# Gates of two token tiles: one-hot products, or added slot by slot into tables in DRAM

## The chip, the cores and the metric

The kernel runs on one core of one Trainium2 chip. A core has five engines with their own instruction queues: TensorE (PE), VectorE (DVE), ScalarE (ACT), GpSimd (POOL) and SyncE (SP), which only issues DMA transfers. ACT and POOL issue transfers too. All move through the core's 16 DMA engines. What counts is the time of one execution in microseconds on the device.

## The reference, cut to what matters

One decoder block over 1024 tokens of width 1024: a mixer made of two gated linear recurrences, then a PEER expert layer, then a norm. The change is in the expert layer. Each token picks, in each of 8 heads, 16 of 16,384 single-neuron experts, so it has 128 slots, each with an expert number and a gate:

```
s_top, i_top = lax.top_k(s, PEER_TOPK)
cand = s_top[:, :, 0, :, None] + s_top[:, :, 1, None, :]
cand_idx = i_top[:, :, 0, :, None] * PEER_N_KEYS + i_top[:, :, 1, None, :]
...
g = jax.nn.softmax(best, axis=-1)
act = jax.nn.gelu(jnp.einsum('td,thkd->thk', xb, u[expert]), approximate=False)
return jnp.einsum('thk,thkd->td', (g * act).astype(xb.dtype), v[expert])
```

An expert number is 128 i + j. The same expert may be picked by several heads of one token; its gates then add up.

## The kernel before, in words

The tokens are 8 tiles of 128; tiles 0 to 3 are the first half, 4 to 7 the second. The mixer runs half by half (projections, attention, output projection), then the scores of the half against the sub-keys, and the selection `select` of experts and gates, which leaves the numbers `e[:, tile]` and the gates `g[:, tile]`.

The expert layer treats the tiles in three ways. For **tiles 0 and 1** the rows of u and v that a token needs are gathered, one slot of a tile at a time: `GatheredTiles.emit` issues an indirect DMA on POOL (line 789) that brings 128 rows of 4 KB, and DVE multiplies and sums them (line 821 for u, 823 for v). For **tiles 3 to 7** all experts are computed densely: for each of 128 columns j, PE multiplies the tokens with 128 rows of u (`DenseProducts`, tile `hps`), the result passes through a gelu, is multiplied with a table of gates, and goes into a second product with rows of v (tiles `sum` and `op`). **Tile 2** (`NG`) is mixed: its u products are gathered like those of tiles 0 and 1, its gates times activations then go into the table of gates, and its v products are dense.

The table `gd` in DRAM holds for each expert row i, tile half, column j and token the gate, zero for nearly all. `scatter_dense` makes it out of one-hot products: for four tokens a step, DVE compares an iota with i (`oi`, line 934) and with j times the gate (`oj`, line 938), PE multiplies the two (`tp`, line 910), ACT copies out (line 911), and ACT's queue stores half a tile at a time. It takes tiles 3, 4, 5, 6, 7 and then 2. Before tile 2 `finish_mixed` issues what is left of its gathered rows.

Three things set the order of the work. The program is recorded in one order for each engine, and every engine keeps it. `Weave` is a planner with assumed costs: a main stream yields steps, and after each the fillers (the gathered rows, the dense columns) may add theirs when none of the planner's clocks runs past the present; `row` and `step` are clocks that only hold a minimum distance. `PACE` gives the distance of gathered rows: 2.4 at first, 14.0 in the second selection and after it, 2.9 and then 4.2 in the expert stage. Gathered rows have six buffers and are used five rows late. Third, waits on semaphores between engines and DMA queues.

While scores, selection and one-hot products of the second half run, dense columns are computed ahead as a filler and spilled to `hd`; the expert stage (`experts`) computes the rest (`fresh`), then reads the spilled ones (`stored`), loads pieces of the table (`gt`, lines 990 and 1009) and ends with `tail`, where the dense tiles get their final norms (line 1127 to 1130) and are stored; the gathered rows that are left come after that, with the final norm of tile 1.

Of the kernel before, what the change touches and what calls it, by code (L numbers as in the profile page):

```python
# [8 lines left out]
F32 = mybir.dt.float32  # L9
F32R = mybir.dt.float32r  # L10
I32 = mybir.dt.int32
U32 = mybir.dt.uint32
AF = mybir.ActivationFunctionType
OP = mybir.AluOpType
# [4 lines left out]
P = 128  # L19
T = 1024  # L20
D = 1024
KD = D // P
HALF = 512
# [10 lines left out]
PACE = (2.4, 14.0, 2.9, 4.2)  # L34
# [717 lines left out]
class GatheredTiles:  # L752
# [16 lines left out]
    def set_pace(self, row):  # L769
        self.options = [Work(dve=1.3, pool=1.1, dma=1.6, row=row)]  # L770
# [4 lines left out]
    def emit(self, w):  # L775
# [21 lines left out]
        if end and kind == "u":  # L797
            self.gate(c)
        elif end:
            nf = self.tile("g_row", ROW_BUFS)  # L800
            nc.sync.dma_start(nf, self.a["norm_f_g"].partition_broadcast(P))
            final_norm(nc, self.pool, self.acc, self.tile("g_hn"), nf, self.out[0, ts, :])
# [4 lines left out]

    def finish_mixed(self):
        options = self.options
        self.set_pace(1.5)  # L810
        while any(c == self.mixed for _, c, _ in self.todo[:1]):
            self.weave.emit(self)
        self.options = options

    def flush(self, keep):
        nc = self.nc
        while len(self.ahead) > keep:
            kind, c, s, row = self.ahead.pop(0)
            act, w = self.act[c][:, s:s + 1], self.g[:, c, s:s + 1]
            if kind == "u":  # L820
                nc.vector.scalar_tensor_tensor(row, row, 1.0, self.hn, OP.mult, OP.mult, accum_out=act)  # L821
            else:
                nc.vector.scalar_tensor_tensor(self.acc, row, w, self.acc, OP.mult, OP.add)  # L823

# [72 lines left out]
def scatter_dense(tc, con, wk, ps, e, weights, tiles, gd, nob, lag, before):  # L897
# [9 lines left out]
    def place(c, tb, t4, ot, oi, oj):  # L907
        pt = ps.tile([P, 4, P], F32, name="tp")
        for q in range(4):
            nc.tensor.matmul(pt[:, q], oi[:, q], oj[:, q], start=True, stop=True)  # L910
        nc.scalar.activation(ot[:, :, t4 * 4:t4 * 4 + 4], pt.rearrange("p t j -> p j t"), AF.Copy)
        if t4 == steps - 1:
            dst = gd[:, (c - NG) * (P // TB) + tb]
            out.extend((dst[:, q:q + 16], ot[:, q:q + 16]) for q in range(0, P, 16))

    ahead, out = [], []
    for c in tiles:
        before(c)
# [50 lines left out]
def experts(tc, a, weave, rows, dense, us, uh, left, right, h_dram, gd, hd, spilled, out):  # L969
# [15 lines left out]
    def paced(ins):  # L985
        tc.add_manual_dep(ins.ins, weave.last.ins.name, nosync(), reason="pace")

    def fresh(j0, n, pool):
        gt = pool.tile([P, nb, n, TB], F32, name="gt", bufs=2)
        paced(nc.sync.dma_start(gt, gd[:, :nb, j0:j0 + n, :]))  # L990
# [16 lines left out]
    def stored(j0, n, gt, raw, pool):  # L1007

        nc.sync.dma_start(gt, gd[:, :nb, j0:j0 + n, :])
# [123 lines left out]
def block_kernel(tc, a, out):  # L1133
    nc = tc.nc
    with ExitStack() as ctx:
# [8 lines left out]
        gd = dram.tile([P, T // TB, P, TB], F32, name="gd")  # L1144
# [39 lines left out]
        with tc.issue_after(pre.ins):  # L1184
            weave.run(attention(tc, con["ident"], cs, 0, mid, wgu, v_d, g_d, (3, 2, 3), mt=hnT))
# [31 lines left out]
        weave.fillers.append(rows)  # L1217
        attn = attention(tc, con["ident"], cs, 1, mid, wgu, v_d, g_d, (3, 2, 3), mt_d)
# [15 lines left out]
        rows.set_pace(PACE[1])  # L1234
        with ExitStack() as c1:
            weave.run(select(tc, left(c1, "sel1", 2), con["iota"], sc_d[1], e[:, 4:], g[:, 4:]))
        with ExitStack() as c1:
            weave.run(scatter_dense(tc, con, left(c1, "sa_wk", 2), left(c1, "sa_ps", 4, space=PSUM),
                                    e, g, [*range(NG + 1, 8), NG], gd, 2, 4,
                                    lambda c: rows.finish_mixed() if c == NG else None))  # L1240

        weave.emit(dense)
        weave.emit(dense)
# [5 lines left out]
        experts(tc, a, weave, rows, dense, us, uh, left, right, h_dram, gd, hd, spilled, out)  # L1249


def prepare(inputs):
    a = {n: np.ascontiguousarray(v) for n, v in inputs.items()}
    a.update(shape_constants())
    a["c_iota"] = np.ascontiguousarray(np.broadcast_to(np.arange(P, dtype=np.float32), (P, P)))
    a["c_sk"] = np.ascontiguousarray(a.pop("peer_sub_keys")[0].reshape(16, P, P).transpose(2, 0, 1))
# [22 lines left out]
```

## Time and profile before

| | |
|---|---|
| three runs | 3472.76, 3458.78 and 5761.45 us |
| median | 3472.76 us |
| the profiled execution | 3467.15 us, span 3465.0 us |
| TensorE's mean granted clock in it | 0.946 of full speed |
| busy share of PE, DVE, ACT, POOL | 91%, 75%, 28%, 31% |
| moved by DMA | 740.18 MB, 214 GB/s |

The span runs from the first to the last instruction of the profiled execution. The run of 5761.45 us stands far from the other two; the profiled execution agrees with those. Busy shares are averages over stages with different limits, so the section with the rows gives tables by stage: there each line is a stretch of time with the busy time of each engine in it. The time that an engine idled before an instruction stands in brackets behind it, with what ended the wait.

### The profile page before, as it was taken

What the parts mean: (1) busy time and instruction counts of PE and PEld (TensorE: products, weight loads), DVE (VectorE), ACT (ScalarE), POOL (GpSimd) and SP (SyncE); (2) the same over time, 40 slices, a digit from 0 to 9 for tenths busy, and PEclk for the clock granted to TensorE, in tenths of its full rate; (3) what the DMA queues carried; (4) which work ended last, traced back from release to release, by engine and by line L of the source; (5) the groups of instructions that cost most, each with busy time, mean ns of one, the idle gap of its engine ahead of it and who ended that gap; (6) DMA issues with size and microseconds to landing.
All of it is one profiled execution on the core that took longest, in us unless ns stands there. A gap on an engine that the chain in (4) does not pass through costs nothing.

```text
span 3465.0 us, 47865 instructions
## 1 busy us (share of the span) xinstructions
PE 3165.9 (91%) x18146; PEld 2814.9 (81%) x18146; DVE 2603.7 (75%) x5465; ACT 966.3 (28%) x1396; POOL 1086.4 (31%) x898
## 2 busy tenths in 40 slices
PE   8998996899778998999869999999999999999992
PEld 8987776787667988999868888888888888788882
DVE  4274499848567698999787777777777777787777
ACT  3241323233122222444332222222222222333320
POOL 2001033313245233000413434444434443322225
PEclk9996998998689999999989999999999999999996
DMA  5301533335589333455858787878887788888876
GB/s 173 114 22 49 182 134 122 103 113 158 192 310 331 116 126 126 167 202 200 319 208 281 261 266 259 275 262 273 268 266 262 265 261 283 301 273 277 269 228 248
DMA packets 347528, 740.18 MB, mean 214 GB/s; under 512 B 23313, under 2 KB 194722, under 8 KB 347042
## 3 DMA queue, kind: packets, MB, share of 16 engines
q0 software_dynamic: 94464, 343.97, 28.7%
q1 hardware_dynamic: 219426, 313.97, 28.2%
q10 hardware_dynamic: 33408, 79.18, 6.0%
q8 instruction: 142, 2.33, 0.3%
q14 instruction: 88, 0.72, 0.1%
HBM read 635.85 MB, written 101.19 MB: 213 GB/s over the span
## 4 chain that ended last, share of the span: by engine, by line
PE 32%; DVE 15%; issue 14%; DMA 8%; POOL 3%; ACT 1%; ACTq 0%; DVEq 0%; POOLq 0%; SPq 0%
DMA raw<-in_c_u_t 4%; PE op L93 4%; PE op L95 4%; PE op L94 4%; PE hps L93 3%; PE hps L94 3%; PE hps L95 3%; PE sum L95 3%; PE sum L93 3%; PE sum L94 3%; DVE g_row L821 2%; POOL g_row L789 2%; DVE ul L83 2%; DVE g_acc L823 2%; DVE acc L1039 1%
## 5 line engine op out<-in xcount | busy, mean ns | idle before, releaser
L789 POOL DMA_INDIRECT g_row<-in_c_u_rows,e x384 | 493.1, 1284 | 1034.9 <-DVE g_row L821 907.4
L93 PE MATMUL hps<-hnTh,uh 128*128 128x320 f32 x2048 | 649.7, 317 | 28.3 <-ACT ht L997 23.4
L95 PE MATMUL hps<-hnTh,ul 128*128 128x320 f32 x2048 | 646.2, 316 | 29.9 <-DVE ul L83 29.9
L94 PE MATMUL hps<-hnTl,uh 128*128 128x320 f32 x2048 | 645.0, 315 | 5.4 <-DVE hnTl L83 5.4
L821 DVE SCALAR_TENSOR_TENSOR g_row<-g_row,g_hn 128x1024 f32<-128x1024 f32 x384 | 466.5, 1236 | 48.3 <-DMA g_row<-in_c_u_rows,e 45.6
L789 POOL DMA_INDIRECT g_row<-in_c_v_rows,e x256 | 325.9, 1273 | 530.0 <-DVE g_acc L823 473.5
L93 PEld LDWEIGHTS hps<-hnTh,uh 128*128 128x128 f32 x2048 | 391.2, 191 | 48.4 <-ACT ht L997 35.7
L95 PEld LDWEIGHTS hps<-hnTh,ul 128*128 128x128 f32 x2048 | 391.3, 191 | 36.5 <-DVE ul L83 32.3
L94 PEld LDWEIGHTS hps<-hnTl,uh 128*128 128x128 f32 x2048 | 391.4, 191 | 12.0 <-DVE hnTl L83 5.8
L823 DVE SCALAR_TENSOR_TENSOR g_acc<-g_row,g,g_acc 128x1024 f32<-128x1024 f32 x256 | 328.0, 1281 | 14.6 <-DMA g_row<-in_c_v_rows,e 10.1
L93 PE MATMUL op<-vh,wh 128*128 128x512 f32 x768 | 307.1, 400 | 24.7 <-DVE acc L1039 24.5
L1039 DVE TENSOR_TENSOR acc<-op,acc 128x512 f32<-128x512 f32 x330 | 226.6, 688 | 133.4 <-PE op L95 125.4
L95 PE MATMUL op<-vh,wl 128*128 128x512 f32 x768 | 303.2, 395 | 0.0
L94 PE MATMUL op<-vl,wh 128*128 128x512 f32 x768 | 301.8, 393 | 0.0
L95 PE MATMUL sum<-vh,wl 128*128 128x512 f32 x768 | 300.5, 392 | 0.0
L94 PE MATMUL sum<-vl,wh 128*128 128x512 f32 x768 | 299.9, 390 | 0.0
L93 PE MATMUL sum<-vh,wh 128*128 128x512 f32 x768 | 299.8, 390 | 0.0
L83 DVE TENSOR_TENSOR ul<-raw,uh 128x1024 fp32r<-128x1024 f32 x128 | 170.8, 1335 | 138.2 <-ACT uh L82 136.2
L82 ACT ACTIVATE uh<-raw 128x1024 fp32r<-128x1024 f32 x128 | 135.6, 1060 | 418.8 <-PE hps L94 237.7
L938 DVE TENSOR_SCALAR oj<-iota,sm 128x128 f32<-128x128 f32 x768 | 226.8, 413 | 0.0
L910 PE MATMUL tp<-oj,oi 128*128 128x128 f32 x1536 | 211.9, 279 | 5.7 <-DVE oj L938 5.5
L910 PEld LDWEIGHTS tp<-oj,oi 128*128 128x128 f32 x1536 | 194.9, 191 | 11.8 <-issue 7.8
(236 smaller groups left out, 6204.8 us busy)
## 6 DMA issues: line engine op xcount, KB each, us to landing
raw<-in_c_u_t SPq DMA_DIRECT2D x128, 512.0 KB
raw<-in_c_v_rows SPq DMA_DIRECT2D x128, 512.0 KB
gd<-ot ACTq DMA_DIRECT2D x96, 512.0 KB
w_raw<-in_w_in SPq DMA_DIRECT2D x28, 1024.0 KB
gt<-gd SPq DMA_DIRECT2D x37, 768.0 KB
gt<-gd SPq DMA_DIRECT2D x18, 1152.0 KB
hd<-ht ACTq DMA_DIRECT2D x112, 160.0 KB
raw<-hd SPq DMA_DIRECT2D x56, 320.0 KB
```

Of the source, the lines that this page charges most:

```text
L82: nc.scalar.activation(hi, src, AF.Copy)
L83: return nc.vector.tensor_sub(lo, src, hi.bitcast(F32))
L93: nc.tensor.matmul(out, l[0], r[0], start=start, stop=False)
L94: nc.tensor.matmul(out, l[0], r[1], start=False, stop=False)
L95: nc.tensor.matmul(out, l[1], r[0], start=False, stop=stop)
L789: load = nc.gpsimd.indirect_dma_start(out=row, out_offset=None, in_=self.rows[kind], in_offset=bass.IndirectOffsetOnAxis(ap=self.e[:, c, s ...
L821: nc.vector.scalar_tensor_tensor(row, row, 1.0, self.hn, OP.mult, OP.mult, accum_out=act)
L823: nc.vector.scalar_tensor_tensor(self.acc, row, w, self.acc, OP.mult, OP.add)
L910: nc.tensor.matmul(pt[:, q], oi[:, q], oj[:, q], start=True, stop=True)
L938: nc.vector.tensor_scalar(oj[:, q], con["iota"], sm[:, 1, t], sm[:, 2, t], OP.is_equal, OP.mult)
L1039: last = nc.vector.tensor_add(acc[c][:, ds], op, acc[c][:, ds])
```

## The change

The tables of tiles 3 and 2 are no longer made by one-hot products. Each gets a table of its own in DRAM (`gd3`, `gd2`), which is filled with zeros from a tile in SBUF while the first half's attention runs. A new filler, `PlacedTiles`, turns the expert numbers of a tile into addresses (four small DVE instructions) and then, for each of 128 slots, issues an indirect DMA on POOL that adds the 128 tokens' gates of that slot, 4 bytes each, to the table. Tile 3 may be placed from the beginning of the second attention; tile 2 when the rows of its u products are all issued. Its planner costs are 1.2 of POOL, 0.8 of DMA and a distance of 2.2. `scatter_dense` keeps tiles 4 to 7. `finish_mixed` goes; the rows of tile 2 get a pace of 4.0 in the second selection, with a DVE cost of 0.4 for the planner, and 14.0 holds from the end of that tile. The expert stage's paces become 2.8 and 3.8. Three dense columns instead of two stand ahead of it, and each load of a piece of the tables becomes three loads.

```diff
-PACE = (2.4, 14.0, 2.9, 4.2)
+PACE = (2.4, 14.0, 2.8, 3.8)
+PACE_MIXED = 4.0
...
         if end and kind == "u":
             self.gate(c)
+            self.set_pace(PACE[1])
...
-    def finish_mixed(self):
-        options = self.options
-        self.set_pace(1.5)
-        while any(c == self.mixed for _, c, _ in self.todo[:1]):
-            self.weave.emit(self)
-        self.options = options
...
+class PlacedTiles:
+    def __init__(self, weave, tc, pool, e, g, c_tok, to, wk, ready):
+        self.weave, self.tc, self.nc, self.e, self.g, self.to, self.wk = weave, tc, tc.nc, e, g, to, wk
+        self.ready = ready
+        self.tok = pool.tile([P, 1], I32, name="tok", bufs=1)
+        tc.nc.sync.dma_start(self.tok, c_tok)
+        self.todo = [(c, s) for c in to for s in range(P)]
+        self.done = False
+        self.work = Work(pool=1.2, dma=0.8, step=2.2)
...
+    def emit(self, w):
+        nc = self.nc
+        c, s = self.todo.pop(0)
+        self.done = not self.todo
+        at = self.e[:, c]
+        if s == 0:
+            col = self.wk[c].bitcast(I32)
+            nc.vector.tensor_scalar(col, at, P - 1, 6, OP.bitwise_and, OP.logical_shift_left)
+            nc.vector.tensor_scalar(at, at, -P, 7, OP.bitwise_and, OP.logical_shift_left)
+            nc.vector.tensor_tensor(at, at, col, OP.bitwise_or)
+            nc.vector.tensor_tensor(at, at, self.tok.to_broadcast([P, P]), OP.bitwise_or)
+        put = nc.gpsimd.indirect_dma_start(
+            out=self.to[c].rearrange("i b j (t o) -> (i b j t) o", o=1),
+            out_offset=bass.IndirectOffsetOnAxis(ap=at[:, s:s + 1], axis=0),
+            in_=self.g[:, c, s:s + 1], in_offset=None, compute_op=OP.add)
+        if self.weave.last:
+            self.tc.add_manual_dep(put.ins, self.weave.last.ins.name, nosync(), reason="pace")
...
+    def gates(gt, js, pace=lambda ins: ins):
+        n = P // TB
+        for c, part in enumerate(gd[:-1]):
+            pace(nc.sync.dma_start(gt[:, c * n:(c + 1) * n], part[:, :, js, :]))
+        pace(nc.sync.dma_start(gt[:, (len(gd) - 1) * n:], gd[-1][:, :, js, :]))
...
-        gd = dram.tile([P, T // TB, P, TB], F32, name="gd")
+        gd_put = {c: dram.tile([P, P // TB, P, TB], F32, name=f"gd{c}") for c in (3, NG)}
+        gd = dram.tile([P, HALF // TB, P, TB], F32, name="gd")
...
+            zero = left(c1, "zero").tile([P, 1024], F32, name="zero")
+            nc.gpsimd.memset(zero, 0.0)
+            for to in gd_put.values():
+                flat = to.rearrange("i b j t -> i (b j t)").rearrange("i (r n) -> i r n", n=1024)
+                nc.sync.dma_start(flat, zero.unsqueeze(1).to_broadcast([P, flat.shape[1], 1024]))
...
+        placed = PlacedTiles(weave, tc, gpool, e, g, a["c_tok"], gd_put, {3: rows.act[0], NG: rows.act[NG]},
+                             lambda c: c != NG or rows.todo[0][1] != NG)
+        weave.fillers.append(placed)
...
-        rows.set_pace(PACE[1])
+        rows.set_pace(PACE_MIXED, 0.4)
...
-                                    e, g, [*range(NG + 1, 8), NG], gd, 2, 4,
-                                    lambda c: rows.finish_mixed() if c == NG else None))
-
-        weave.emit(dense)
-        weave.emit(dense)
+                                    e, g, range(4, 8), gd, 2, 4))
+
+        weave.finish(placed)
+        for _ in range(3):
+            weave.emit(dense)
```

Where the recorded order moves. In the rows below the lines of the changed kernel are one higher than before (790 for 789, 526 for 525, 670 for 669); `g_row` is a gathered row, `gd_68` the table of tile 3, `gd_69` that of tile 2.

POOL in the second attention, before, where `o_rs` and `o` are the norm of a chunk's output and its gating:

```order
L73 TENSOR_TENSOR o_rs<-o_ms,power 128x4
L525 TENSOR_TENSOR o<-o,gt 128x512
L789 DMA g_row<-in_c_u_rows,e 128x1024 x3
L73 TENSOR_TENSOR o_rs<-o_ms,power 128x4
L789 DMA g_row<-in_c_u_rows,e 128x1024
```

And now:

```order
L74 TENSOR_TENSOR o_rs<-o_ms,power 128x4
L851 DMA gd_68<-g,e 2097152x1
L526 TENSOR_TENSOR o<-o,gt 128x512
L851 DMA gd_68<-g,e 2097152x1
L790 DMA g_row<-in_c_u_rows,e 128x1024
L851 DMA gd_68<-g,e 2097152x1
L790 DMA g_row<-in_c_u_rows,e 128x1024
L851 DMA gd_68<-g,e 2097152x1
```

Adds stand between rows, norms and gatings, one at a time here; up to the first work for the second selection there are 112 of them and 108 rows, before 104 rows.

POOL from the last head of the second selection on, before (`eq` and `ce` are its products and sums):

```order
L654 TENSOR_TENSOR ce<-ixf 128x4x6
L657 TENSOR_TENSOR ce<-ixf 128x4x8
L669 TENSOR_TENSOR eq<-eq,ce 128x1600 x2
L789 DMA g_row<-in_c_u_rows,e 128x1024 x280
L789 DMA g_row<-in_c_v_rows,e 128x1024 x129
```

And now:

```order
L658 TENSOR_TENSOR ce<-ixf 128x4x8
L851 DMA gd_69<-g,e 2097152x1 x2
L670 TENSOR_TENSOR eq<-eq,ce 128x1600
L851 DMA gd_69<-g,e 2097152x1
L670 TENSOR_TENSOR eq<-eq,ce 128x1600
L851 DMA gd_69<-g,e 2097152x1 x91
L790 DMA g_row<-in_c_u_rows,e 128x1024 x256
L790 DMA g_row<-in_c_v_rows,e 128x1024 x130
```

Inside the selection there are now 53 adds and 20 rows; 91 adds follow it in one run, and the gathered rows of tiles 0 and 1 come behind them. Each add waits for the semaphore of the add before it, as the same part of the new order with its waits shows (`DMASW` are the semaphores that POOL's transfers take in turn):

```order
L851 DMA gd_69<-g,e 2097152x1 [waits DMASW2_49]
L851 DMA gd_69<-g,e 2097152x1 [waits DMASW3_49]
L851 DMA gd_69<-g,e 2097152x1 [waits DMASW4_49]
L851 DMA gd_69<-g,e 2097152x1 [waits DMASW5_49]
L851 DMA gd_69<-g,e 2097152x1 [waits DMASW6_49]
```

SP at the first load of a piece of the table, before (`raw` are u and v for a dense column):

```order
L847 DMA raw<-in_c_u_t 128x1024 x37
L993 DMA raw<-in_c_v_rows 128x1024
L783 DMA g_hn<-hn_dram 128x1024
L847 DMA raw<-in_c_u_t 128x1024
L993 DMA raw<-in_c_v_rows 128x1024
L990 DMA gt<-gd 128x12x128
```

And now:

```order
L880 DMA raw<-in_c_u_t 128x1024 x31
L1032 DMA raw<-in_c_v_rows 128x1024
L1024 DMA gt<-gd_69 128x2x128
L1024 DMA gt<-gd_68 128x2x128
L1025 DMA gt<-gd 128x8x128
L880 DMA raw<-in_c_u_t 128x1024
L1032 DMA raw<-in_c_v_rows 128x1024
```

The load from `gd_69` waits for the last add, and all later loads of SP stand behind it. On PE 52.5 instead of 58.5 dense columns stand ahead of the first v product; 306 dense matmuls, of 48 a column, lie between the last one-hot product and that product, and 5.9 columns up to the place at which PE waited for the table before. 50 columns instead of 56 are spilled.

## Rows read from the trace of the kernel before

**Rows 1.** The page: span, and busy time and instructions of each engine.
```profile
span 3465.0 us, 47865 instructions
PE 3165.9 (91%) x18146; PEld 2814.9 (81%) x18146; DVE 2603.7 (75%) x5465; ACT 966.3 (28%) x1396; POOL 1086.4 (31%) x898
```

**Rows 2.** By stage: length, busy us (instructions) of each engine, clock, DMA share, GB/s.
```profile
160.00:215.00 55.00, 51.90 (x312) 44.86 (x311) 32.00 (x76) 19.39 (x36) 1.76 (x2) 0.97 0.05 16
...
1150.00:1376.00 226.00, 203.47 (x1338) 200.20 (x1336) 214.53 (x936) 52.75 (x92) 85.80 (x75) 0.98 0.38 120
1376.00:1673.00 297.00, 294.35 (x2244) 289.87 (x2245) 288.62 (x842) 129.94 (x224) 4.23 (x4) 0.98 0.54 198
1673.00:1727.00 54.00, 42.10 (x275) 41.44 (x274) 36.10 (x57) 13.13 (x21) 35.06 (x23) 0.87 0.94 358
1727.00:1783.00 56.00, 50.04 (x381) 47.84 (x380) 55.29 (x164) 21.96 (x38) 1.50 (x2) 1.00 0.37 142
...
1850.00:2950.00 1100.00, 1081.43 (x5798) 951.81 (x5797) 841.55 (x1165) 260.37 (x353) 468.04 (x360) 1.00 0.81 268
2950.00:3401.00 451.00, 448.29 (x1942) 365.28 (x1941) 354.70 (x384) 135.88 (x166) 123.38 (x105) 0.99 0.79 261
3401.00:3465.00 64.00, 1.39 (x7) 0.80 (x5) 45.32 (x40) 2.49 (x6) 38.98 (x33) 0.54 0.81 290
```

**Rows 3.** In order of time: start, length, instruction, [idle before, what ended it]; SP, PE.
```profile
1790.03 0.38 SPq L990 DMA_DIRECT2D gt<-gd  x1
...
1803.86 0.64 PE L93 MATMUL hps<-hnTh,uh 128*128 128x320 f32 x1 [23.42 <-ACT ht L997]
```

**Rows 4.** By line: operation, count, busy us, mean ns, idle before.
```profile
L789 POOL DMA_INDIRECT g_row<-in_c_u_rows,e x384 | 493.1, 1284 | 1034.9 <-DVE g_row L821 907.4
...
L821 DVE SCALAR_TENSOR_TENSOR g_row<-g_row,g_hn 128x1024 f32<-128x1024 f32 x384 | 466.5, 1236 | 48.3 <-DMA g_row<-in_c_u_rows,e 45.6
...
L669 POOL TENSOR_TENSOR eq<-eq,ce 128x1600 f32<-128x1600 f32 x32 | 131.5, 4123 | 85.6 <-DVE eq L667 79.4 <-DVE x_ms L71 6.2
```

**Rows 5.** In order of time: the end of the program.
```profile
3398.20 2.01 POOL L789 DMA_INDIRECT g_row<-in_c_v_rows,e  x1 [0.17 <-issue]
...
3404.59 1.28 DVE L823 SCALAR_TENSOR_TENSOR g_acc<-g_row,g,g_acc 128x1024 f32<-128x1024 f32 x1 [0.16 <-DMA g_row<-in_c_v_rows,e]
...
3407.33 1.28 DVE L1129 SCALAR_TENSOR_TENSOR raw<-acc,f_rs,nf 128x1024 f32<-128x1024 f32 x1 [1.39 <-POOL f_rs L73]
...
3447.88 1.01 POOL L789 DMA_INDIRECT g_row<-in_c_v_rows,e  x1 [0.30 <-issue]
3449.19 1.02 POOL L789 DMA_INDIRECT g_row<-in_c_v_rows,e  x1 [0.31 <-issue]
...
3454.95 1.28 DVE L823 SCALAR_TENSOR_TENSOR g_acc<-g_row,g,g_acc 128x1024 f32<-128x1024 f32 x1 [0.95 <-DMA g_row<-in_c_v_rows,e]
3456.48 1.28 DVE L823 SCALAR_TENSOR_TENSOR g_acc<-g_row,g,g_acc 128x1024 f32<-128x1024 f32 x1 [0.24 <-DMA g_row<-in_c_v_rows,e]
...
3461.12 0.33 SPq L1130 DMA_DIRECT2D out_dram<-g_hn  x1
```

**Rows 6.** In order of time: SP, the fourth gate load of the first attention.
```profile
215.59 0.52 SPq L494 DMA_DIRECT2D gt<-g_d  x1
```

**Rows 7.** In order of time: a store on SP, and ACT's next use of its tile.
```profile
3397.30 0.34 SPq L1130 DMA_DIRECT2D out_dram<-raw  x1
...
3400.03 1.07 ACT L1127 ACTIVATE raw<-acc 128x1024 f32<-128x1024 f32 x1 [3.93 <-DMA out_dram<-raw]
```

**Rows 8.** In order of time: POOL's first gather, and its first work in the second selection.
```profile
743.09 3.53 POOL L789 DMA_INDIRECT g_row<-in_c_u_rows,e  x1 [64.94 <-PE pp L95]
...
1167.75 2.26 POOL L651 TENSOR_TENSOR ce<-ixf 128x64 f32<-128x64 f32 x5 [53.64 <-DVE ixf L644]
```

**Rows 9.** In order of time: POOL and DVE where the mixed tile's last rows begin.
```profile
1673.78 1.68 POOL L789 DMA_INDIRECT g_row<-in_c_u_rows,e  x1 [292.63 <-DVE g_row L821]
1675.76 7.89 POOL L789 DMA_INDIRECT g_row<-in_c_u_rows,e  x1 [0.30 <-issue]
...
1681.42 1.43 DVE L821 SCALAR_TENSOR_TENSOR g_row<-g_row,g_hn 128x1024 f32<-128x1024 f32 x1
```

## What the change will do to the time

> **What bounds the kernel now.** I read the busy times of the page first, then the table of stages, then single stretches. TensorE (PE) is busy for 3165.9 of 3465.0 us [rows 1], so an edit can only win where PE idles or does work that can go. The stages [rows 2] show three kinds of stretch. In the expert stage PE is the bound: 1081.43 of 1100 us and 448.29 of 451. While the one-hot products of five tiles run, from 1376 to 1673 us, PE and VectorE (DVE) are both full, 294.35 and 288.62 of 297. Before it, in the second selection, DVE is the bound with 214.53 of 226. Then there are three holes: 54 us in which the last 24 rows of the mixed tile are gathered (PE 42.10), 56 us for the products of that tile, and a wait for its table, after which PE resumes at 1803.86 having idled 23.42 us, 13.8 us after the first table load was issued at 1790.03 [rows 3]. At the end PE has 1.39 us of work in the last 64 us: gathered rows and their final norm trail alone.
>
> **What the change removes.** Two of six tiles of one-hot products. The five tiles took 297 us, 59.4 each, so four take 238. The 24 rows and the mixed tile's products leave the path. Counted to the moment at which PE resumes on the first products that need the tables: the selection ends at 1376 before; 20 mixed rows now stand inside it, and DVE there has no room, so 20 x 1.24 us [rows 4] = 25 us longer; then 238 us; then the dense products that the order puts between the last one-hot product and that moment, 5.9 expert columns. A dense column costs PE 7.6 us: a fresh column takes 15.9 (1100 us for 5798 matmuls at 84 a column) and a stored one 8.35 (1942 matmuls at 36 a column in 451 us) [rows 2]. That gives 45 us, and 1376 + 25 + 238 + 45 = 1684 in place of 1804: **120 us gained, if the adds are done in time**.
>
> **What it gives back.** Only 50 columns are spilled early instead of 56, so six more run in the expert stage: 6 x 7.6 = 46 us. The rest of that stage is PE's, unchanged, and the rows there, 512 now, take the same 1.24 us of DVE each beside 77% busy DVE, so I cost the slightly denser pace at nothing; the cover is PE's own time, and if DVE or the DMA engines (0.81 busy) fill, each lost percent of PE there costs 16 us. The three smaller table loads replace one on SP's queue and are issued a group ahead: nothing.
>
> **The tail.** In the new order all gathered rows stand ahead of the final norms of the dense tiles. The last of those ended at 3407.33 + 1.28 us, and a store took 3.9 us from its issue to the end of the span (3461.12 to 3465.0) [rows 5], so the program could end at about 3412.5 instead of 3465.0: 53 us gained.
>
> **The zeros.** The two tables need 16.8 MB of zeros, on SP's queue ahead of the load that stood at 215.59 [rows 6]. The DMA engines are 0.05 busy there; at the 358 GB/s of another stretch [rows 2] they take 47 us, which fits before that load. It can cost 0 to 25 us if they run slower; I take 8.
>
> **The adds, on which all depends.** 256 adds are issued from POOL, and each waits for the previous one's semaphore, so they form a chain. No row shows an add. From below, two indirect DMAs that don't wait on each other start 1.25 to 1.5 us apart; from above, a gather of 512 KB was issued at 3398.20 and its row used at 3404.59, 6.4 us [rows 5]. Nearer is a 512 KB store: issued at 3397.30, it freed its tile for ScalarE at 3400.03, 2.73 us [rows 7]. Replacing SP's issue (0.34) by POOL's mean 1.28 [rows 4] gives 3.67. Of that the data are up to 1.53 us (two gathered rows landed at 3454.95 and 3456.48), and an add has 512 bytes: 2.14. An add also has to read the table, which the store did not, and other traffic is in the way. Between 2.14 and 3.67, I take **3.2 us**, nearer the upper value, as an estimate.
>
> The Trainium skill ("DMA: Bandwidth & Descriptors", Anatomy of one DMA) puts a fixed 2.0 us on every DMA that GpSimd issues, most of it the wait until the write is confirmed. By that figure alone the chain would run at about 2 us and be hidden everywhere; the sum would be 3346.
>
> The chain has three stretches. (1) From the first gather at 743.09 to POOL's first work for the selection at 1167.75 [rows 8] there are 425 us, and the order holds 112 adds: 112 x 3.2 = 358. The 108 rows between them are issued while adds land. It fits, with 67 us for rows that wait for DVE. What queues behind a waiting add there is the output norm of the attention and its gate; I cost that at nothing as long as the spare lasts. (2) In the selection POOL has 53 adds (68 us of issue), 20 rows (26), 8 heads of two products at 4.12 us [rows 4] and small sums of 2.7 us, five of the seven in 2.26 [rows 8] (87 in all), and 30 adds directly behind an add, which wait 3.2 - 1.28 each (58): 239 us, against 226 + 25 for DVE. Both are nearly full and wait on each other, the products for DVE and DVE for the products; I take 15 us. (3) 91 adds follow in one run: 291 us, against 238 us of one-hot products and 45 - 14 = 31 us of dense work before the table load must go out: 22 us late. SP's queue holds the later expert loads behind that load, so PE idles for it.
>
> **The sum.** 3465 - 120 + 46 - 53 + 8 = 3346 with the adds hidden; + 15 + 22 = 3383. The median of the runs, 3472.76, is 7.8 above this span, so 3391: about **3390**.
>
> **Rivals.** What a measurement of this kernel can tell from no change is 2%: below 3403 is faster, above 3542 slower.
>
> *The forecast*, a period of at most 3.33 us, span up to 3395: chance 0.45. *Better*, the adds below 3.0 us, and the scores stage relieved because rows and adds now share time that was filled with gathers: down to 3330, chance 0.05.
>
> *The chain is late.* At 3.6 us stretch (3) alone is 59 us late: 3346 + 15 + 59 = 3420. At 4.0 it is 95, the selection 12 and stretch (1) 24: 3492. Break-even is about 3.85. For it speaks that the data's share of 2.73 us may be small and that gathers in this kernel take 6.4. Chance of 3.33 to 4.2: 0.27, within 2%. Above 4.2, by the same sum 3550 and more: 0.05, slower.
>
> *POOL is starved, the slower side.* At 1675.76 the issue of a gather took 7.89 us instead of about 1, and it ended one issue's length after a row of DVE products without gaps that began its last piece at 1681.42 [rows 9]. In the one-hot stage DVE is busy for 288.62 of 297 us, so the 91 adds may get in only when that stage is over. Then they start there: 91 x 3.2 - 31 = 260 us late, 3346 + 15 + 260 = 3621. It decides from about 33 of the 91 adds left over (104 us), where the time is that of before. Against it: in the expert stage, with DVE 77% busy, gathers were issued in 1.28 us on average [rows 4], and the row ahead of the long one took 1.68 in the same stretch. No gather was issued inside the one-hot stage, so the trace does not decide. Chance 0.18. The Trainium skill ("SBUF — State Buffer", Who interferes with whom) states it as a rule: GpSimd's descriptors wait while DVE holds the shared port, as it does in single-source fp32 products with both operands in SBUF and, for reads, in products of two SBUF tensors; by that rule the one-hot stage is such a place, and the row of 7.89 us agrees.
>
> That the change doesn't do what it says is contained in these: the one-hot work goes, but the wait for the chain takes its place.
>
> **The range.** 3325 to 3575: the forecast, the better case, the late chain and the nearer third of the starved case; what is left out is most of the starved case and the top of the slow chain, under 0.2. The forecast's own range is 3345 to 3403. Faster by over 2%: 0.45 + 0.05 = 0.50. Within 2%: 0.27. Slower: 0.18 + 0.05 = 0.23.
>
> **What would show it.** In the new trace: distances of adds in the run of 91, at about 3.2 us or not; when the last add lands against the end of the one-hot products (forecast: about 50 us after it); PE's idle time before the first expert product (forecast 20 to 40 us); the one-hot stage at 238 us and the selection at about 250; length of POOL's add issues inside the one-hot stage (about 1.3 us, or many); stage lengths up to 1150 us unchanged but for about 8 us of zeros; and the time between PE's last product and the end, about 11 us in place of 64. It is wrong if the chain's period is not near 3.2 us, if DVE shuts POOL out, or if the gathers, which all start after the last add, no longer end before the last norms.

## The result, and the profile after

The changed kernel takes 3690.72 us (median of 4 runs) against 3469.45 us, a ratio of 1.0639 (95% interval 1.0595 to 1.0683). It is 6.4% slower; 3390 had been forecast, and the range ended at 3575. One run of each kernel stood far above the others (4436.53 and 5761.45 us), and the ratio leaves these two out.

The page of the changed kernel, which answers to [rows 1]:

```profile
span 3688.0 us, 46854 instructions
PE 3129.0 (85%) x17628; PEld 2772.8 (75%) x17628; DVE 2498.6 (68%) x5159; ACT 925.9 (25%) x1326; POOL 1505.4 (41%) x1155
```

PE does 37 us less work in 223 us more: the time is idle time. The table of stages says where. Its columns are those of [rows 2]; the stretches are from the first add to the selection, the selection, the one-hot products, and the wait for the table:

```profile
747.00:1312.00 565.00, 398.85 (x2002) 339.96 (x2002) 310.55 (x661) 120.43 (x196) 362.64 (x248) 0.78 0.62 179
1312.00:1620.00 308.00, 189.12 (x1177) 186.22 (x1177) 213.64 (x862) 50.31 (x84) 193.06 (x149) 0.80 0.44 114
1620.00:1844.00 224.00, 223.58 (x1737) 219.80 (x1736) 222.68 (x652) 101.66 (x175) 86.34 (x50) 1.00 0.59 185
1844.00:2013.00 169.00, 41.88 (x287) 41.62 (x286) 17.24 (x21) 15.43 (x22) 72.41 (x48) 0.63 0.36 96
```

Only the third line looks like [rows 2]: PE and DVE full, 56 us a tile. In the first two neither is full, and POOL is busy for 363 of 565 us. What it does with the rest stands in the groups by line for 743 to 1312 us (count, busy time, mean ns, idle time before them and what ended it):

```profile
L851 POOL DMA_INDIRECT gd<-g,e x112 | 201.5, 1800 | 164.4 <-DMA gd<-g,e 147.9 <-issue 16.1 <-DVE st L514 0.3
L790 POOL DMA_INDIRECT g_row<-in_c_u_rows,e x108 | 134.1, 1242 | 97.1 <-PE pp L96 64.9 <-issue 25.9 <-DVE g_row L816 3.8
```

The 112 adds take POOL 201.5 + 164.4 us, the rows 134.1 + 32 (without the 64.9 before the first). With 37 us of norms, gatings and stores that is 569 us; the lines overlap a little, and the stretch has 565, so this is all that there is. POOL waits for other engines for only some 10 us of it. DVE waits for POOL instead, in the same stretch (us in total, times, longest):

```profile
DVE g_row L816 <- DMA g_row<-in_c_u_rows,e: 125.8, 53, 21.4
DVE o L525 <- POOL o_rs L74: 36.5, 8, 8.8
```

In the kernel before, from the first gather to the selection, POOL had waited for DVE, and DVE little for POOL:

```profile
POOL g_row L789 <- DVE g_row L821: 131.0, 45, 28.5
DVE g_row L821 <- DMA g_row<-in_c_u_rows,e: 31.0, 26, 6.3
DVE o L524 <- POOL o_rs L73: 6.0, 8, 1.2
```

A row's product stands in DVE's fixed order for a row that POOL should have issued earlier; while DVE stands there, the attention stands. In the selection, the second line of the table, 193 us of work and a wait of 88.5 us at the adds, for which 58 had been counted, take 282 of POOL's 308 us:

```profile
POOL gd L851 <- DMA gd<-g,e: 88.5, 40, 4.9
```

The run of 91 adds, in order of time, once the other engines are out of work (start, length, idle time before and its end), then SP's load of the table and PE's first product behind it, which answer to [rows 3]:

```profile
1888.55 1.55 POOL L851 DMA_INDIRECT gd<-g,e  x1 [1.73 <-DMA gd<-g,e]
1891.67 1.55 POOL L851 DMA_INDIRECT gd<-g,e  x1 [1.58 <-DMA gd<-g,e]
1894.91 1.55 POOL L851 DMA_INDIRECT gd<-g,e  x1 [1.69 <-DMA gd<-g,e]
...
1980.47 1.55 POOL L851 DMA_INDIRECT gd<-g,e  x1 [1.73 <-DMA gd<-g,e]
```

```profile
1983.55 1.18 SPq L1024 DMA_DIRECT2D gt<-gd  x2
```

```profile
2012.90 0.64 PE L94 MATMUL hps<-hnTh,uh 128*128 128x320 f32 x1 [127.12 <-ACT ht L1036]
```

From 1888.55 to 1980.47 lie 28 periods of 3.28 us each: the chain without traffic is what was forecast. But the one-hot products have ended at 1844, and PE idles for 127 us. While these products ran, the adds were further apart, 50 of them in 224 us, 4.5 us each; the lines below them give the median time from issue to landing there and from 1888 us on:

```profile
L851 POOL DMA_INDIRECT gd<-g,e x50 | 86.3, 1727 | 137.3 <-DMA gd<-g,e 137.3
...
gd<-g,e POOLq DMA_INDIRECT x50, 3.5
...
gd<-g,e POOLq DMA_INDIRECT x29, 3.0
```

The tail has gone as forecast: the last final norm ends 6.6 us before the span of 3688.0 does, and no gathered row comes behind it ([rows 5]):

```profile
3680.09 1.28 DVE L1168 SCALAR_TENSOR_TENSOR raw<-acc,f_rs,nf 128x1024 f32<-128x1024 f32 x1 [0.73 <-POOL f_rs L74]
```

### The profile page after: what moved, and what is told of

Its sections match the earlier page's. It is cut to its first block, busy times and chain, and to the rows that moved or that the text cites. A ratio compares the mean times of both kernels' runs of the same rounds, so it can differ in the third digit from the quotient of the medians.

```text
span 3688.0 us, 46854 instructions
## 1 busy us (share of the span) xinstructions
PE 3129.0 (85%) x17628; PEld 2772.8 (75%) x17628; DVE 2498.6 (68%) x5159; ACT 925.9 (25%) x1326; POOL 1505.4 (41%) x1155
## 5 line engine op out<-in xcount | busy, mean ns | idle before, releaser
L790 POOL DMA_INDIRECT g_row<-in_c_u_rows,e x384 | 480.2, 1250 | 546.7 <-DVE g_row L816 407.6
L851 POOL DMA_INDIRECT gd<-g,e x256 | 443.8, 1734 | 472.5 <-DMA gd<-g,e 450.6
L84 DVE TENSOR_TENSOR ul<-raw,uh 128x1024 fp32r<-128x1024 f32 x128 | 159.3, 1245 | 147.8 <-ACT uh L83 147.8
L94 PEld LDWEIGHTS op<-vh,wh 128*128 128x128 f32 x768 | 144.5, 188 | 87.8 <-DVE acc L1078 61.1
L95 PE MATMUL pp<-w_lo,xh 128*128 128x256 f32 x704 | 197.6, 281 | 3.7 <-DVE w_lo L84 3.7
```

What stands on the lines that cost most here:

```text
L84: return nc.vector.tensor_sub(lo, src, hi.bitcast(F32))
L94: nc.tensor.matmul(out, l[0], r[0], start=start, stop=False)
L95: nc.tensor.matmul(out, l[0], r[1], start=False, stop=False)
L790: load = nc.gpsimd.indirect_dma_start(out=row, out_offset=None, in_=self.rows[kind], in_offset=bass.IndirectOffsetOnAxis(ap=self.e[:, c, s ...
L851: put = nc.gpsimd.indirect_dma_start(out=self.to[c].rearrange("i b j (t o) -> (i b j t) o", o=1), out_offset=bass.IndirectOffsetOnAxis(ap= ...
```

## The experiments

Times are medians; a ratio is to the kernel before, run beside each kernel. Landmarks of the profiled runs, in us: POOL's first work for the second selection, the first and the last one-hot product, the first expert product (`sum`) and the last (`op`), and the span. "Ahead" is the number of dense columns spilled ahead; the names stand at the experiments below.

| kernel | selection | one-hot | `sum` | `op` | span | ahead | time |
|---|---|---|---|---|---|---|---|
| before | 1168 | 1391–1780 | 1810 | 3402 | 3465 | 56 | 3469 |
| after | 1313 | 1620–1844 | 2019 | 3676 | 3688 | 50 | 3691 |
| no_adds | 1172 | 1424–1647 | 1692 | 3359 | 3368 | 50 | 3377 |
| paces_only | 1168 | 1391–1780 | 1809 | 3423 | 3450 | 56 | 3449 |
| adds_apart | 1316 | 1601–1824 | 1869 | 3530 | 3543 | 50 | 3546 |
| heads | 1305 | 1593–1817 | 1862 | 3526 | 3538 | 50 | 3543 |
| same_order | 1217 | 1494–1717 | 1762 | 3422 | 3435 | 50 | 3440 |
| heads_late | 1230 | 1505–1729 | 1813 | 3441 | 3471 | 56 | 3472 |
| heads_thin | 1202 | 1458–1681 | 1801 | 3451 | 3468 | 54 | 3468 |
| heads_even | 1194 | 1446–1668 | 1791 | 3435 | 3452 | 54 | 3457 |
| heads_balanced | 1215 | 1465–1687 | 1745 | 3431 | 3451 | 48 | 3453 |
| tile3_spread | 1216 | 1436–1765 | 1797 | 3450 | 3463 | 52 | 3468 |
| tile3_heads | 1165 | 1385–1710 | 1743 | 3400 | 3413 | 52 | 3418 |
| tile3_chain | 1158 | 1377–1820 | 1851 | 3511 | 3524 | 52 | 3523 |

**Without the adds (no_adds).**

```diff
-        put = nc.gpsimd.indirect_dma_start(
-            out=self.to[c].rearrange("i b j (t o) -> (i b j t) o", o=1),
-            out_offset=bass.IndirectOffsetOnAxis(ap=at[:, s:s + 1], axis=0),
-            in_=self.g[:, c, s:s + 1], in_offset=None, compute_op=OP.add)
```

> The changed kernel with its 256 adds left out (the tables of tiles 3 and 2 stay zero, so the gates of these two tiles are missing from the dense sum); every other instruction keeps its place in the order. Theory A: all that the change lost is the adds, as work in POOL's in-order queue and as a chain that SP waits for. Then this kernel shows what the prediction had with the adds hidden, a span of 3346 us, time about 3354 us. Theory B: the zeros, the three table loads, the six columns and the denser pace of rows cost what was lost. Then it stays above 3500 us. In between, each has its part: after minus this run is the price of the adds.

Measured 3376.83 us, ratio 0.9741 (0.9714 to 0.9769). So the adds cost 3690.7 - 3376.8 = 314 us, and what was forecast for the rest, 3354, lacks 23. Theory A holds; part of the 23 is in the third experiment.

**The adds in eight tables (adds_apart).**

```diff
+        k = s % 8
         put = nc.gpsimd.indirect_dma_start(
-            out=self.to[c].rearrange("i b j (t o) -> (i b j t) o", o=1),
+            out=self.small[k].rearrange("r (n o) -> (r n) o", o=1),
```

> The 256 adds stay where they are in POOL's order, but go into eight small tables of 0.5 MB in turn (their addresses cut to 17 bits), so that an add waits for the one eight back instead of the one before it, and the loads of the two large tables, which stay zero, wait for no add: the gates of tiles 3 and 2 are missing. Theory A1, the wait from add to add is what costs: POOL's own issue (256 x 2.0 us with the gap behind it) fits beside the other work but for some 30 us in the selection, time 3360 to 3420 us. Theory A2, the issue on POOL alone fills its queue: in the stretch up to the selection, 112 adds x 2.0 + 108 rows x 1.55 = 391 us of the 425 of before, plus the norms and gatings behind them; the stages before the one-hot products stay late by over 100 us, time above 3450 us.

Measured 3546.47 us, 1.0227 (1.0197 to 1.0257). The wait at the expert stage is gone (`sum` 45 us behind the last one-hot product, as without adds), but the one-hot products still start at 1601. By its text that speaks for A2, and I took it so at first. It was no clean test: without the waits the recorded order moves too, with 73 adds instead of 50 ahead of the last norm of the attention, in bursts.

**The paces alone (paces_only).**

```diff
-PACE = (2.4, 14.0, 2.9, 4.2)
+PACE = (2.4, 14.0, 2.8, 3.8)
```

> The kernel before with only the two paces of the expert stage changed, 2.8 and 3.8 for 2.9 and 4.2. Theory A: the gathered rows then end with the dense products, the tail of 64 us falls to about 11, and the stage itself, which TensorE sets, does not get longer: 3470 - 50 = about 3420 us. Theory B: denser rows make the expert stage longer by as much as the tail gets shorter (after had 1676 us from its first product of that stage to its last, against 1600 before, with six columns more): 3460 us or more.

Measured 3449.35 us, 0.9950 (0.9926 to 0.9974): between the two. The time behind the last expert product falls from 63.5 to 26.7 us, but the stage from `sum` to `op` grows from 1591.9 to 1614.4. Of these 22 us PE's waits for the sums on DVE show 18 (24.5 us before, in the same stage):

```profile
PE op L93 <- DVE acc L1039: 42.4, 40, 3.7
```

**Half of the change, thinly spread (tile3_spread).**

```diff
+        placed = PlacedTiles(weave, tc, gpool, e, g, a["c_tok"], gd_put, {3: rows.act[0]}, lambda c: True)
...
-                                    e, g, [*range(NG + 1, 8), NG], gd, 2, 4,
+                                    e, g, [4, 5, 6, 7, NG], gd, 2, 4,
```

> Half of the change, thinly spread: the kernel before with the new paces, in which only tile 3 gets its gates by 128 adds, at a distance of 6.0 instead of 2.2 for the planner (56 before the second selection, 29 in it, 39 in the one-hot stage, 4 after), while tile 2 stays mixed with its one-hot products at the end. Theory A: an add costs nothing where POOL has room and nobody waits behind it, so one tile of one-hot products less is worth 59 us, the tail 53, less about 30 for columns that are no longer spilled: 3470 - 82 = about 3390 us. Theory C: each add costs its share of what 256 cost wherever it stands (after minus the run without adds, halved, some 170 us): 3530 us or more.

Measured 3467.96 us, 1.0006 (0.9990 to 1.0022). Neither theory. Against the paces alone, 85 chained adds ahead of the one-hot products make these 45 us late, 60 us of products are saved, and the expert stage is 38 us longer with four columns more in it, with 14 us less behind it. Against the kernel before nothing is left.

**A wait at each head only (heads).** A token's 16 experts of one head differ, and each token has its own elements of the table, so only adds of different heads can meet. The Trainium skill ("DMA: Bandwidth & Descriptors", Rules for kernel authors) asks that an accumulating DMA wait for the semaphore of an earlier access of the same bytes; by that, 7 waits a tile are needed, at the beginnings of heads, and not 127.

```diff
+        if s % 16 == 0:
+            for other in heads[-1] if heads else []:
+                self.tc.add_manual_dep(put.ins, other.ins.name, sync(), reason="next head")
+        else:
+            for other in heads[-1]:
+                self.tc.declare_no_dep(put.ins, other.ins, reason="other addresses")
```

> The changed kernel, complete, in which an add waits only where its head of 16 slots begins: within a head a token's 16 experts differ, so the addresses do too. The first add of a head waits for all 16 of the head before. In POOL's order the adds move forward, since nothing holds them: 84 instead of 64 stand ahead of the last norm of the second attention. Theory: the wait for the table before the expert stage goes (129 us), and the lateness up to the one-hot products (195 us) stays, because it comes from adds issued ahead of the norms, gates and products of other stages on POOL; time about that of the adds in eight small tables, 3550 us. Rival: the waits from add to add made the early stages late too, and the small tables hid that by an extra cost of their own; then about 3400 us.

Measured 3542.95 us, 1.0216 (1.0199 to 1.0234), the time that the theory had; whether its reason holds is for the run with the same places below. Counted exactly, 73 adds instead of 50 stand ahead of the last norm; 84 and 64 is the count up to the first store behind the attention. What makes the attention late is seen in its timeline and in DVE's waits from 747 to 1025 us:

```profile
754.21 1.58 POOL L856 DMA_INDIRECT gd<-g,e  x1 [0.30 <-issue]
756.09 2.07 POOL L856 DMA_INDIRECT gd<-g,e  x1 [0.30 <-issue]
...
779.81 1.55 POOL L856 DMA_INDIRECT gd<-g,e  x1 [0.30 <-issue]
781.67 1.01 POOL L794 DMA_INDIRECT g_row<-in_c_u_rows,e  x1 [0.30 <-issue]
```

```profile
DVE o L529 <- POOL o_rs L78: 78.8, 8, 30.2
```

An unchained add costs POOL 1.85 us, 0.30 of it between two issues, where nothing holds it up; a burst of 14 adds, the first at 752.28 us, stands ahead of everything else at 2.1 us an add, and DVE waits up to 30 us for a norm.

**No adds in the attention (heads_late).**

```diff
             weave.run(attn)
+        weave.fillers.append(placed)
...
-        self.work = Work(pool=1.2, dma=0.8, step=2.2)
+        self.work = Work(pool=1.2, dma=0.8, step=2.4)
```

> As the kernel before this one (a wait at each head only), but the adds may start only after the second attention's stream, at a planner distance of 2.4, and rows and adds keep their order among themselves on POOL: 12 instead of 64 adds stand ahead of the last norm of the attention, 60 up to the selection, 70 in it, 114 in one run behind it. Theory: what counts is whether POOL's queue has room where the adds stand. Attention as without adds; between it and the selection 60 x 1.86 + 60 x 1.55 = 205 us of the 240 there; in the selection 70 x 1.86 + 31 + 87 = 248 us of 252; the run of 114 x 1.86 = 212 us is over before the one-hot products and dense columns behind them end (268 us). So about the kernel without adds plus 20 to 40 us: 3395 to 3420 us, faster than before by 2%. Rival: an add costs 0.6 to 0.7 us of the end wherever it stands (170 us for 256 in the small tables): 3540 us.

Measured 3471.72 us, 1.0006 (0.9995 to 1.0018): a miss, and not the rival either. In fact no add stood ahead of the last norm. The attention ends as without adds (last norm at 930.7, there 934.2), but the selection begins 58 us late and takes 22 longer: the room on POOL was overestimated, by counting 1.86 us an add and 1.55 a row and nothing for what waits behind them.

**Thinner, and evenly spread (heads_thin, heads_even).** In both the distance is 1.9 behind the selection.

```diff
-step=2.4
+step=3.5   # heads_thin
+step=5.0   # heads_even, from the second attention's beginning
```

> As the version with a wait at each head and no adds during the attention, but thinner: planner distance 3.5 up to the end of the selection and 1.9 behind it. 10 adds during the attention, 41 between it and the selection (60 before), 55 in the selection (70), 150 in one run behind it (114). Theory: what POOL has to issue between attention and selection falls by 19 x 1.86 = 35 us, in the selection by 28 us, so the one-hot products start some 60 us earlier than in the denser version, at about 1445; the run of 150 x 1.86 = 280 us then ends at 1725, about 5 us before the table load is needed behind the one-hot products and the dense columns. Time about 3395 to 3425 us, below both kernels and below the one with only the paces changed (3449). Rival: POOL's place in the order is not what made the selection late there (its DMA traffic or DVE's shared port was); then the start of the one-hot products moves by less than 25 us, 3450 us or more.

> The same, spread evenly from the beginning of the second attention at a planner distance of 5.0: 38 adds in the attention, 29 between it and the selection, 38 in it, 151 in the run behind it. Theory: POOL has the same work before the one-hot products, but in the attention norms and gates wait for at most one add (1.9 us, sixteen times on a chain of eight chunks), so the attention ends 10 to 20 us later and the rest is relieved by 23 more adds: between 10 us better and 10 us worse than the thin version. Rival: every add ahead of a norm costs its full issue, 38 x 1.86 = 70 us later at the end of the attention.

Measured 3468.1 us (1.0000, 0.9980 to 1.0019) and 3456.72 us (0.9961, 0.9939 to 0.9983); the first is a miss, and the second, 11 us better, lies at the edge of what was forecast. The one-hot products of the thin version start 46 us earlier than those of the version before it, at 1458, near the forecast 1445. But its run of 150 adds then ends last, and SP's load goes out right behind it:

```profile
L860 POOL DMA_INDIRECT gd<-g,e x150 | 255.9, 1706 | 64.3 <-issue 43.0 <-DMA gd<-g,e 21.0 <-DVE ul L88 0.3
```

```profile
1770.48 1.18 SPq L1046 DMA_DIRECT2D gt<-gd  x2
```

150 adds took 320 us, 2.13 each, where 280 were expected. In the evenly spread version 32 adds ahead of the last norm of the attention made it 5 us later than without, not 70.

**The same places, without the chain (same_order).** As the version with a wait at each head, but the adds are recorded at the places that they have in the changed kernel (`ORDER` is that sequence):

```diff
+    def flush(self, after):
+        while self.planned:
+            n = SPOTS["A"][len(self.puts)]
+            while self.head < n and (self.head in self.seen or ORDER[self.head] == "A"):
+                self.head += 1
+            if self.head < n:
+                return
+            self.one(*self.planned.pop(0), after)
```

> The changed kernel, complete, with a wait at each head only, and with the adds held at the places of POOL's order that they have in the changed kernel (64 of them before the first store of the second attention's rows, 48 from there to the selection, 57 instead of 53 in it, 87 in the run behind). So only the waits from add to add are gone: in the changed kernel POOL idled 148 us for them between 743 and 1312 us and 86 us in the selection. Theory W, these waits made the early stages late: POOL's issue alone then just fits, the one-hot products start at 1470 to 1500 instead of 1620, nothing waits at the expert stage, time 3420 to 3470 us. Theory I, the issue alone makes them late: the start stays at 1580 or more, and the time is that of the version with a wait at each head and its own order, 3540 us.

Measured 3440.08 us, 0.9921 (0.9891 to 0.9950): theory W. It splits the price: 3690.7 - 3440.1 = 251 us for the waits from add to add, 3440.1 - 3376.8 = 63 us for the issue of 256 adds (by the ratios, since these runs were not made side by side, 249 and 62). The one-hot products start at 1494 instead of 1620, and the 129 us more behind them are gone too. Against the version with a wait at each head, which differs from this one only in the places of the adds, it is 103 us faster. So that version was late for another reason than the changed kernel, its bursts, and its time did not show what the waits cost; its rival, that the waits made the early stages late, is right in the main. POOL's waits from 743 to 1312 us, where the changed kernel had 147.9 us at adds:

```profile
POOL gd L895 <- DMA gd<-g,e: 7.6, 3, 3.6
```

**Half of the change, without the chain (tile3_heads, tile3_chain).** The kernel of the fourth experiment with a wait at each head and a distance of 12, then 1.9 behind the selection; and, as its counterpart, the same order with each add waiting for the one before.

```diff
-step=6
+step=12
...
+        placed.work = Work(pool=1.2, dma=0.8, step=1.9)
```

> Half of the change with a wait at each head: the kernel before with the new paces, tile 3 placed by 128 adds, 12 of them before the last norm of the attention, 26 more up to the end of the selection, 90 in one run under the one-hot products of four tiles; tile 2 stays mixed with its one-hot products at the end. Theory: the run takes 90 x 2.0 = 180 us of the 225 there, nobody waits for it, and few adds stand ahead of other work; so the expert stage begins 45 to 57 us earlier than with the paces alone, which gives back about 30 us for four columns that are no longer spilled early, and its tail is 10 to 15 us shorter: 3449 - 57 + 30 - 12 = about 3410 to 3435 us. Rival: one-hot products less give nothing at all, since PE fills the time with columns that it would have computed anyway: 3445 to 3455 us.

> The kernel with tile 3 alone placed by 128 adds (38 before the one-hot products, 90 in one run under them), in the same order on POOL, but with each add waiting for the one before it again. Theory: few adds stand ahead of other work, so the one-hot products start within 20 us of the version with a wait at each head (1385); the run takes 90 x 4.1 = 370 us instead of 166, and the mixed tile's last rows, which stand behind it on POOL, come only at 1755 instead of 1551, so the expert stage begins some 120 us later than there (1736): 3418 + 120 = about 3540 us. Rival: with half of the adds the chain hides behind the one-hot products; within 25 us of 3418 us.

Measured 3417.89 us, 0.9857 (0.9827 to 0.9887), and 3523.42 us, 1.0149 (1.0116 to 1.0182). The first is faster than both kernels, by 1.4% against the one before: clear of the noise, but inside the 2% that the prediction counts as no change. The adds from 1380 us on, first of the one, then of the other:

```profile
L865 POOL DMA_INDIRECT gd<-g,e x86 | 145.5, 1692 | 26.9 <-issue 25.7 <-DMA gd<-g,e 1.2
```

```profile
L865 POOL DMA_INDIRECT gd<-g,e x85 | 141.4, 1663 | 197.3 <-DMA gd<-g,e 197.3
```

Same issue, 2.0 and 4.0 us apart. Nobody waits for the adds while the one-hot products run, but the mixed tile's last rows stand behind them on POOL: they come at 1717 instead of 1551, and everything after is 108 us later. So the rival, that half a chain hides, falls, and the gain of this kernel hangs on the missing waits. In the first of the two DVE was busy for 233 of 240 us meanwhile, and the adds were issued all the same:

```profile
1385.00:1625.00 240.00, 231.83 (x1788) 227.66 (x1787) 233.05 (x673) 103.06 (x178) 157.23 (x97) 0.99 0.69 209
```

**Balanced (heads_balanced).** Distance 4.0 from the second attention on, 1.9 behind the selection.

```diff
-step=5.0
+step=4.0
```

> Both tiles placed with a wait at each head, planner distance 4.0 from the second attention on and 1.9 behind the selection: 46 adds up to the attention's end, 38 up to the selection, 48 in it, 124 in the run. Theory: POOL has 256 x 1.9 to 2.0 us of issue to do between 747 us and the table load, whatever the places; what counts is that neither the stages before nor the run are overfull. The run of 124 x 1.95 = 242 us is over within the one-hot products and the dense columns behind them (268), the one-hot products start at 1460 to 1490 us: 3415 to 3445 us, between the evenly spread version (3457) and the run without adds (3377). Rival: the run is not what held the evenly spread version back; then no better than 3450 us.

Measured 3452.84 us, 0.9947 (0.9930 to 0.9964): a miss; the time is the rival's, but not its reason. The front is as forecast (one-hot products from 1465, `sum` at 1745, 46 us before the evenly spread version), but the expert stage takes 1686 us instead of 1644. Six columns fewer spilled are 6 x 7.6 = 46 us by the forecast's price, 42 as measured: what the front gains PE pays there. No complete version with both tiles placed came near the one without adds; the best is the one with the same places, 3440.

## Why the prediction was wrong, step by step

**The step that failed** is the pricing of the chain: a distance of adds, "Between 2.14 and 3.67, I take 3.2 us", was set against the length of each stretch as if POOL had nothing else to do, with "The 108 rows between them are issued while adds land", "It fits, with 67 us for rows that wait for DVE", "I cost that at nothing as long as the spare lasts", 15 us for the selection and 22 for the run. 3.2 is right for a chain that has POOL and the DMA engines to itself (3.28), in part by luck, since it was picked between two far bounds. The three stretches, against the kernel without adds; the last column is the run with the same places, in which only the waits from add to add are gone:

| stretch | forecast | measured | without the waits |
|---|---|---|---|
| to the selection | 0 | 1313 - 1172 = 141 us | 45 |
| the selection, to the first one-hot product | 15 | 307 - 252 = 55 us | 25 |
| from there to the first expert product | 22 | 399 - 268 = 131 us | 0 |

In the first, the price of the adds themselves was right: 201.5 + 164.4 us for 112 is 3.27 each, 366 us, where 358 had been forecast. The overlap was not. POOL issues one thing at a time, 1.80 us an add and 1.24 a row with mostly 0.30 between two, and the chain's waits shrink only where a row stands between two adds. So the 166 us of the rows and the 37 of the norms, gatings and stores, taken at nothing, come on top, and the sum is what the stretch took. In the second, POOL was nearly full in the same way, and the waits at adds were 88.5 us instead of 58. In the third the adds were 4.1 us apart on average, 1610.42 to 1980.47 for 91, because they landed later while the one-hot products ran (median 3.5 us, 3.0 alone); the sum with this distance is 91 x 4.1 - 269 = 104 us late. Another 16 lie behind the load of the table: from its issue to PE's first product it took 29.4 us (1983.55 to 2012.90), where the 13.8 of the kernel before had been carried over [rows 3].

**The rivals.** "The chain is late" was the right one in kind, with too small a price: it knew only the distance of adds, not the queue, and gave 3550 at a period above 4.2. "POOL is starved" falls. In the one-hot stage of the changed kernel the issue of an add took 1.73 us, 1.55 with DVE idle, the longest 3.33, and none stood until the stage was over. The Trainium skill ("SBUF — State Buffer", Who interferes with whom) would have had POOL wait there; of that the runs show 0.2 us an add. The row of 7.89 us, from which the rival was drawn, was no sample of that stage: beside it DVE ran products of two tensors at 1.43 us each [rows 9], and in the one-hot stage most of its instructions are far shorter:

```profile
L970 DVE TENSOR_SCALAR oj<-iota,sm 128x128 f32<-128x128 f32 x508 | 144.1, 350 | 0.0
L966 DVE TENSOR_TENSOR oi<-iota,sm 128x512 f32<-128x512 f32 x126 | 85.6, 679 | 1.3 <-ACT sm L960 1.2
```

What held that row was not tried. The rule of the Trainium skill's "DMA: Bandwidth & Descriptors" (Anatomy of one DMA), 2.0 us for each DMA from GpSimd, gave 3346; an add landed 3.0 us after its issue began at the median of the undisturbed run, so the measurement speaks against it here.

**What held.** The front, in the kernel without adds: `sum` 117 us earlier (forecast 120). The tail, from the last expert product to the end: shorter by 53.6 us without adds, by 51 in the changed kernel (forecast 53). The one-hot stage of four tiles: 224 us (238). Zeros: POOL's first gather starts 4 us later, at 747.08 (8); the kernel before and the one with only its paces changed differ as much there (743.09 and 739.0).

**A second, smaller miss:** "I cost the slightly denser pace at nothing". The paces alone lengthened the stage by 22 us, through DVE's sums that PE waits for; six columns and these 22 us are 68 of the 74 us by which the stage of the kernel without adds is longer than before.

**Not settled:** which traffic delays an add. Its landing was later in every busy stretch, but no run took one transfer away, and DVE is busy in the same stretches; that the traffic does it is argued, not shown.

## What to carry to other kernels

A chain of small dependent transfers costs its issue on the engine that sends them, for everything queued behind, and its waits as well where the queue is in order: add up the whole queue of that engine stretch by stretch, not the chain's period. Ask which of the waits the data need: here 7 of 127 a tile, and the others were 251 of the 314 us that the adds cost. Ask also where the issues stand: the same adds with the same waits differed by 103 us between two orders. Work that shortens a stage in whose shadow other work is done ahead gives part of its gain back later, at the price of that work (7.6 us a column by the forecast, 7 to 11 where the runs differ in columns).

## What the runs showed of the hardware

- An accumulating indirect DMA of 128 x 4 bytes into DRAM takes POOL 1.55 us to issue at least, where a gather of 128 rows takes about 0.95. Chained, such adds are 3.28 us apart undisturbed and 4.0 to 4.5 in the one-hot stage of these kernels; unchained, 1.85 undisturbed and 2.0 to 2.13 in the one-hot stage.
- The mean granted clock of PE was 0.78 and 0.80 of its upper level (2.4 GHz) in the two late stretches of the changed kernel, in which PE idled 166 of 565 and 119 of 308 us, 1.00 in the one-hot stage and 0.63 while it waited for the table. A mean below 1.00 says that part of these stretches ran at the lower level (1.2 GHz); what that cost no run priced apart.
